# A hybrid decoder layer: two small casts change engines, and a scan's second tile gets a scheduling step of its own

## The chip, the cores and the metric

The kernel runs on one core of a Trainium2 chip. A core has engines that work side by side, each through its own queue in order: TensorE (PE in the profile; its weight loads are PEld), VectorE (DVE), ScalarE (ACT), GpSimd (POOL), and SyncE (SP), which here only issues DMA transfers. They wait for each other through semaphores. PE reads from SBUF and writes to PSUM; DVE and ACT read and write both. The metric is the time of one execution on the device in microseconds (us); a run's time is compared with others as a median of several.

## What is computed

One layer of a decoder over 16 meta tokens and 512 tokens, 1024 wide, in float32. Cut to what matters here:

```python
u = rmsnorm(h, mix_norm_w)
proj = u @ w_in                      # pool, z, xbc, dt, gates
xbc = silu(causal_depthwise_conv(xbc, conv_w, conv_b))        # 4 taps
xs, b_mat, c_mat = split(xbc)        # 32 heads of 64; 8 groups of state 128
dt = softplus(dt_raw + dt_bias);  a = -exp(a_log)
# chunks of 128 tokens, the 16 meta tokens a leading chunk of their own
y_diag = einsum("bclsg,bclsgr,bcsgrp->bclgrp", c.b, exp(a_l - a_s), x*dt)
states = einsum("bclgn,bclgr,bclgrp->bcgrpn", b, exp(a_end - a), x*dt)
prev   = scan over chunks: h = chunk_decay * h + states
y_off  = einsum("bclgn,bcgrpn,bclgr->bclgrp", c, prev, exp(a))
y = y_diag + y_off + xs * d_skip
yg = y * silu(z);  yg = yg * rsqrt(mean(yg**2 over the group) + eps) * norm_w
h = h + (gate_pool * y_pool + gate_ssd * (yg @ w_ssd_out)) @ w_o
h = h + relu(rmsnorm(h) @ w_ff1)**2 @ w_ff2
```

y_pool is a causal mean over 2 to 16 tokens, less the token itself, through two matrices. The output is the normalised h without the meta tokens.

## The kernel before

Matrices are multiplied with operands in two parts: a value rounded to the matrix type (`hi`, made by a cast on ACT) and what is missing (`lo`, a subtraction on DVE); three products of these (`whi`, `wlo` for a block of weights, `uh`, `ul` for the activations) make one. A block of weights is 128 x 1024; `block_part` (lines 72 to 76) loads it into `raw` (three buffers), casts it (L75) and subtracts (L76).

The scan goes group by group (eight groups of four heads), in the loop at lines 577 to 583. While the scan of group g is computed, the projections of group g+1 fill PE. Both are Python generators, `ssd` and `group_proj`, and `weave` takes one step of each in turn: a step ends at a `yield`. `group_proj` has a step for each of its tiles: bt (B), ct (C), the two halves of xc (x), then, for groups 1, 2, 3 and 5, a gate (pgp), and z (two blocks into pz, silu into zt). A tile's projection (px) ends in its convolution, `conv`: one tap on ACT (L340), three on DVE (L343), which read px in PSUM, and a silu on ACT (L345). For g = 4 the first half of the output projection (pso) is filled in as well, with two steps to one of the scan; for g = 7 the fill is the output projection of groups 4 to 6 (psp, `out_part`).

The steps of `ssd`:

1. abc, the running sums of the decay, is loaded and spread over the partitions. Transposes on PE: ptb (B in tokens; btok, bm), ptm and ptx (x in tokens; xdm, xm, xdt). The meta tokens' operands are stacked three times into 80 partitions: `bm` as hi, hi, lo and `xm` as hi, mid, hi, so that one product gives the sum of three. xdd is xdt times a decay; eb and abc are exponentials on ACT.
2. pcb = B times C, masked into cbm; the chunk states: pst from bm and xm for the meta tokens (L462), from btok and xdd for three chunks (L464); st is the running state (L466 on ACT, L468 and L469 on DVE); abc is multiplied with cbm (L470).
3. po = states times C (L478), py = xdt times abc (L484), each in two tiles; then four DVE instructions on each tile, the additions: yt = po * eb, + py, + xc * d_skip, * zt (L488 to L492).
4. The group norm: sq (L496, L497), its two parts qh and ql.
5. png, a sum over partitions by PE (L501, L502); the root rs on ACT (L504), four reciprocals on DVE (L506).
6. yt times norm weight and rs (L510); yh and yl, its two parts for the output projection (L513, L514).

What order the instructions take on each engine isn't the program's order. The Tile framework's scheduler works through the whole program with estimates of its own and puts an instruction into its engine's queue when it finds it ready; program order only gives the priority. So a `yield` that moves changes the priority of all that stands behind it. On the chip the queue is fixed, and an instruction that waits holds up all behind it on its engine.

PSUM has two buffers of two banks (px, pz, pso, psp, pgp) and four of one bank (ptb, ptm, ptx, pcb, pst, po, py, png). ACT loads a table (ACT_TABLE_LOAD) whenever its next function needs another one: root, exponential, silu and sigmoid each change it here.

Of the kernel before, what the change touches and what calls it, by code (L numbers as in the profile page):

```python
# [51 lines left out]
def kernel(ctx: ExitStack, tc, xT, x, w, vec, fnw, out):  # L52
    nc = tc.nc
    act, dve, pe, pool = nc.scalar, nc.vector, nc.tensor, nc.gpsimd
# [77 lines left out]
    xm = gc.tile([MQ, R, HEAD], F32R, name="xm", bufs=1)  # L132
# [55 lines left out]
    b, raw, hi, lo = wdt  # L188
# [200 lines left out]
    def bc(ap, n):  # L389
        return ap.unsqueeze(len(ap.shape)).to_broadcast(list(ap.shape) + [n])  # L390

    def ssd(g, cur):
# [10 lines left out]
        xdm = gs.tile([NM, R, 64], F32, tag="xdm", name=f"xdm{g}")  # L403
# [6 lines left out]
        hi, mid, low = slice(0, NM), slice(32, 32 + NM), slice(64, 64 + NM)  # L410
# [5 lines left out]
        for i in range(2):  # L416
            pe.transpose(pm[:NM, i * P : (i + 1) * P], xc[:, i, :NM], ident)
        dve.tensor_tensor(xdm, pm[:NM, :256].rearrange("p (r d) -> p r d", r=R),
                          bc(decm[:, hs], 64), op=ALU.mult)
        act.copy(xm[hi], xdm)  # L420
        act.copy(xm[low], xdm)
        dve.tensor_tensor(xm[mid], xdm, xm[hi].bitcast(F32), op=ALU.subtract)
        for b in range(2):
            pt = psum1(f"ptx{g}_{b}")
# [61 lines left out]
        for i in range(2):  # L486
# [3 lines left out]
            dve.scalar_tensor_tensor(y, xc[:, i, NM:], col(V_DS, 2 * g + i), y,  # L490
                                     op0=ALU.mult, op1=ALU.add)
            dve.tensor_tensor(y, y, zt[:, i, :], op=ALU.mult)  # L492
        yield

        sq = gs.tile([P, 2, SEQ], F32, tag="eb", name=f"sqg{g}")
        act.activation(sq, yt, AF.Square)  # L496
# [80 lines left out]
    for g in range(G):  # L577
        nxt = group_tiles(g + 1) if g + 1 < G else None
        fill = [group_proj(g + 1, nxt, GATE_AT.get(g))] if nxt else [out_part()]
        if g == 4:  # L580
            fill = [out_half()] + fill
        weave(ssd(g, cur), fill, 2 if g == 4 else 1)
        cur = nxt
# [638 lines left out]
```

## Time and profile before

| what | value |
|---|---|
| median of 3 runs | 1037.89 us (1037.26 to 1038.09) |
| profiled execution | 1037.43 us |
| its span, first to last instruction | 1035.7 us |
| mean granted clock of PE | 0.996 |
| the scan's groups (the weave) | about 66 to 500 us of the span |

In the page, a group of instructions is named by line, engine, operation and out<-in with the program's tile names; buffer numbers are left out, so px is any projection. A time line's row has start, duration, engine, line, operation, tiles, shapes, count, and in square brackets the idle time of the engine just before it and who ended it. A row of waits has the total, how often, and the longest. In a row of windows each engine has its busy time and its count; behind POOL stand the granted clock of PE, the DMA share and GB/s.

### The profile page before, as it was taken

Reading aid. Unit: us, or ns where it says so; the run is one execution under the profiler, and the core shown is the slowest. Engines: PE = TensorE matmul, PEld = TensorE weight load, DVE = VectorE, ACT = ScalarE, POOL = GpSimd, SP = SyncE. Lnnn points to the kernel's source line nnn. Section 1 sums busy time; section 2 is a strip of 40 time slices with the busy share of each in tenths; the row PEclk is TensorE's granted clock in tenths of the full one; section 3 lists DMA queues with packets and bytes.
Section 4 is the critical chain, followed back from the end, with each engine's and each line's share of the span. In section 5 each row is a group of like instructions: output and inputs, shape, how many; then the busy total and the mean of one; then the engine's idle time right before and its main releaser. Section 6 shows DMA issues by size and latency. Waiting matters only on the chain.

```text
span 1035.7 us, 14112 instructions
## 1 busy us (share of the span) xinstructions
PE 1011.8 (98%) x5689; PEld 875.4 (85%) x5689; DVE 737.1 (71%) x966; ACT 565.2 (55%) x756; POOL 88.6 (9%) x52
## 2 busy tenths in 40 slices
PE   9999899989899998999999999999999999999997
PEld 9889899879689997988899888888888888888886
DVE  7978787768645585878656557875777667666866
ACT  7776757667736439493234333465455345454444
POOL 0100000000000000000000000102131412403400
PEclk9999999999999999999999999999999999999999
DMA  6243142222233330504623333324323323334112
GB/s 237 84 143 102 32 132 84 100 87 97 84 123 100 90 113 2 166 18 122 224 85 99 102 102 87 137 68 156 102 82 122 102 83 121 97 107 119 43 43 82
DMA packets 29282, 105.64 MB, mean 102 GB/s; under 512 B 3296, under 2 KB 4256, under 8 KB 28192
## 3 DMA queue, kind: packets, MB, share of 16 engines
q1 hardware_dynamic: 26496, 92.75, 28.0%
q0 software_dynamic: 2000, 11.08, 3.0%
q8 instruction: 45, 0.74, 0.3%
q10 hardware_dynamic: 720, 0.91, 0.2%
q14 instruction: 21, 0.17, 0.0%
HBM read 102.55 MB, written 2.16 MB: 101 GB/s over the span
## 4 chain that ended last, share of the span: by engine, by line
PE 84%; ACT 9%; DVE 4%; issue 2%; DMA 0%; DVEq 0%; ACTq 0%
PE pf L93 6%; PE pf L92 6%; PE pf L94 6%; PE px L150 5%; PE px L153 5%; PE px L151 5%; PE alpha L971 3%; PE alpha L972 3%; PE alpha L973 3%; PE py L484 2%; PE pz L153 2%; PE pz L150 2%; PE pz L151 2%; PE pp L153 1%; PE pp L151 1%
## 5 line engine op out<-in xcount | busy, mean ns | idle before, releaser
L75 ACT CAST whi<-raw 128x1024 fp32r<-128x1024 f32 (+1 forms) x131 | 135.6, 1042 | 220.8 <-PE pf L93 55.8
L76 DVE TENSOR_TENSOR wlo<-raw,whi 128x1024 fp32r<-128x1024 f32 (+1 forms) x131 | 163.6, 1253 | 106.1 <-ACT whi L75 106.0
L150 PE MATMUL px<-uh,whi 128*128 128x264 f32 (+1 forms) x448 | 120.4, 289 | 5.9 <-ACT whi L75 3.0
L151 PE MATMUL px<-ul,whi 128*128 128x264 f32 (+1 forms) x448 | 118.0, 284 | 0.0
L92 PE MATMUL pf<-vh,whi 128*128 128x512 f32 x256 | 99.8, 390 | 0.0
L94 PE MATMUL pf<-vh,wlo 128*128 128x512 f32 x256 | 99.6, 389 | 0.0
L93 PE MATMUL pf<-vl,whi 128*128 128x512 f32 x256 | 99.6, 389 | 0.0
L150 PEld LDWEIGHTS px<-uh,whi 128*128 128x128 f32 x448 | 84.9, 189 | 9.0 <-ACT whi L75 4.8
L153 PE MATMUL px<-uh,wlo 128*128 128x264 f32 (+1 forms) x448 | 90.7, 285 | 1.1 <-DVE wlo L76 1.1
L151 PEld LDWEIGHTS px<-ul,whi 128*128 128x128 f32 x448 | 84.7, 189 | 0.3 <-issue 0.2
L733 DVE TENSOR_TENSOR slo<-b,shi 128x1024 fp32r<-128x1024 f32 x35 | 49.2, 1405 | 31.6 <-ACT shi L732 31.6
L153 PEld LDWEIGHTS px<-uh,wlo 128*128 128x128 f32 x448 | 68.7, 188 | 2.0 <-DVE wlo L76 1.5
L732 ACT CAST shi<-b 128x1024 fp32r<-128x1024 f32 x35 | 36.7, 1048 | 47.3 <-PE pf L93 36.4
L94 PEld LDWEIGHTS pf<-vh,wlo 128*128 128x128 f32 x256 | 48.0, 188 | 10.1
L92 PEld LDWEIGHTS pf<-vh,whi 128*128 128x128 f32 x256 | 48.0, 188 | 10.0
L93 PEld LDWEIGHTS pf<-vl,whi 128*128 128x128 f32 x256 | 48.1, 188 | 9.9
L982 POOL TENSOR_TENSOR b<-b,b 128x1024 f32<-128x1024 f32 x14 | 35.6, 2540 | 238.4 <-DVE slo L733 210.2
L971 PE MATMUL alpha<-shi,hh 128*128 128x512 f32 x140 | 54.6, 390 | 0.0
L972 PE MATMUL alpha<-slo,hh 128*128 128x512 f32 x140 | 54.5, 389 | 0.0
L973 PE MATMUL alpha<-shi,hl 128*128 128x512 f32 x140 | 54.5, 389 | 0.0
L798 DVE TENSOR_TENSOR ht<-ht,alpha 128x1024 f32<-128x1024 f32 x35 | 42.6, 1217 | 10.9 <-PE alpha L973 10.9
L150 PE MATMUL pz<-uh,whi 128*128 128x512 f32 x112 | 43.9, 392 | 0.0
(419 smaller groups left out, 2527.8 us busy)
## 6 DMA issues: line engine op xcount, KB each, us to landing
raw<-in_w SPq DMA_DIRECT2D x129, 512.0 KB, 3.6
b<-in_w SPq DMA_DIRECT2D x28, 512.0 KB, 3.6
abc<-acs_d POOLq DMA_DIRECT2D x8, 1024.0 KB, 5.0
wob<-in_w SPq DMA_DIRECT2D x8, 512.0 KB, 6.0
xt<-in_xT SPq DMA_DIRECT2D x8, 264.0 KB, 5.3
ht<-in_x POOLq DMA_DIRECT2D x4, 512.0 KB, 6.3
w<-in_w SPq DMA_DIRECT2D x4, 512.0 KB, 3.5
out_dram<-out SPq DMA_DIRECT2D x4, 320.0 KB, 2.4
```

Of the source, the lines that this page charges most:

```text
L75: act.copy(hi[:, c], raw[:, c])
L76: dve.tensor_tensor(lo[:, c], raw[:, c], hi[:, c].bitcast(F32), op=ALU.subtract)
L92: pe.matmul(ps, ah, bh, start=first, stop=False)
L93: pe.matmul(ps, ah, bl, start=False, stop=False)
L94: pe.matmul(ps, al, bh, start=False, stop=last)
L150: pe.matmul(o, wh, rhs[0][k][:, c], start=k == 0, stop=False)
L151: pe.matmul(o, wh, rhs[1][k][:, c], start=False, stop=False)
L153: pe.matmul(o, wl, rhs[0][k][:, c], start=False, stop=k == NK - 1)
L733: dve.tensor_tensor(lo, src, hi.bitcast(F32), op=ALU.subtract)
L971: pe.matmul(ps[t], a[0], wh[:, cs], start=f, stop=False, skip_group_check=True)
L972: pe.matmul(ps[t], a[0], wl[:, cs], start=False, stop=False, skip_group_check=True)
L973: pe.matmul(ps[t], a[1], wh[:, cs], start=False, stop=l, skip_group_check=True)
```

## The change

Two edits in `ssd`. The two casts of xdm into `xm` (lines 420 and 421) are issued by DVE instead of ACT. And the `yield` behind the additions moves into their loop, so that the step ends after the additions of tile 0 and again after those of tile 1: the scan has seven steps instead of six, and everything from the second tile's additions on comes one step of the fill later.

```diff
@@ -417,8 +417,8 @@
         dve.tensor_tensor(xdm, pm[:NM, :256].rearrange("p (r d) -> p r d", r=R),
                           bc(decm[:, hs], 64), op=ALU.mult)
-        act.copy(xm[hi], xdm)
-        act.copy(xm[low], xdm)
+        dve.tensor_copy(xm[hi], xdm)
+        dve.tensor_copy(xm[low], xdm)
         dve.tensor_tensor(xm[mid], xdm, xm[hi].bitcast(F32), op=ALU.subtract)
@@ -490,7 +490,7 @@
             dve.scalar_tensor_tensor(y, xc[:, i, NM:], col(V_DS, 2 * g + i), y,
                                      op0=ALU.mult, op1=ALU.add)
             dve.tensor_tensor(y, y, zt[:, i, :], op=ALU.mult)
-        yield
+            yield
 
         sq = gs.tile([P, 2, SEQ], F32, tag="eb", name=f"sqg{g}")
```

What the scheduler makes of it, in the instruction order. Names carry buffer numbers here: rs0 is group 0's root, xdm1 group 1's operand, whi17 the weight block of number 17. First ACT where the scan of group 0 ends and that of group 1 begins. Before, from the root of group 0 on:

```order
L504 ACT_TABLE_LOAD
L504 ACTIVATE rs0_1192<-png0_1189,eps_83 128x512
L439 ACT_TABLE_LOAD
L439 ACTIVATE eb1_1309<-abc1_1274 64x1024
L345 ACT_TABLE_LOAD
L345 ACTIVATE xc1_820<-xc1_820 128x528
L444 ACTIVATE abc1_1274<-abc1_1274,dtok_87 128x128 x3
L513 CAST yh0_0_1261<-yt0_1025 128x512
L385 ACTIVATE zt1_823<-pz1_1198 128x1024
L513 CAST yh0_1_1266<-yt0_1025 128x512
L409 COPY btok1_1278<-ptb1_1279 128x384
L412 CAST bm_114<-ptb1_1279 16x128
```

Now the root stands behind the exponential of abc and behind zt, and ahead of it stand the same table load and eb as above, and one Relu:

```order
L345 ACT_TABLE_LOAD
L345 ACTIVATE xc1_820<-xc1_820 128x528
L444 ACTIVATE abc1_1274<-abc1_1274,dtok_87 128x128 x7
L450 ACT_TABLE_LOAD
L450 ACTIVATE abc1_1274<-abc1_1274 128x1024
L385 ACT_TABLE_LOAD
L385 ACTIVATE zt1_823<-pz1_1189 128x1024
L504 ACT_TABLE_LOAD
L504 ACTIVATE rs0_1254<-png0_1251,eps_83 128x512
L409 COPY btok1_1278<-ptb1_1279 128x384
L412 CAST bm_114<-ptb1_1279 16x128
L413 CAST bm_114<-ptb1_1279 16x128
```

The root has moved behind eb, xc, the exponential of abc and zt, each with its table load. Next DVE at the same place. Before, from the subtraction that completes bm to the first state sum:

```order
L414 TENSOR_TENSOR bm_114<-ptb1_1279,bm_114 16x128
L422 TENSOR_TENSOR xm_115<-xdm1_1277,xm_115 16x256
L429 TENSOR_TENSOR xdt1_1276<-ptx1_1_1301,dtok_87 128x512
L447 TENSOR_SCALAR abc1_1274<-abc1_1274,dtok_87 128x128
L433 TENSOR_TENSOR xdd1_1307<-xdt1_1276,dec_89 128x768
L457 TENSOR_TENSOR cbm1_1395<-pcb1_1390,tri_78 128x512
L343 SCALAR_TENSOR_TENSOR bt2_1271<-px2_18_1330,vs_85,bt2_1271 128x527
L470 TENSOR_TENSOR abc1_1274<-abc1_1274,cbm1_1395 128x2048
L343 SCALAR_TENSOR_TENSOR bt2_1271<-px2_18_1330,vs_85,bt2_1271 128x526
L468 TENSOR_TENSOR st1_1_1398<-st0_1_1397,cdec_90 128x256
L343 SCALAR_TENSOR_TENSOR bt2_1271<-px2_18_1330,vs_85,bt2_1271 128x525
L469 TENSOR_TENSOR st1_1_1398<-st1_1_1398,pst1_0_1401 128x256
```

Now, to the same state sum:

```order
L506 RECIPROCAL rs0_1254<-rs0_1254 128x128 x4
L414 TENSOR_TENSOR bm_114<-ptb1_1279,bm_114 16x128
L510 SCALAR_TENSOR_TENSOR yt0_1025<-yt0_1025,vs_85,rs0_1254 128x512 x2
L343 SCALAR_TENSOR_TENSOR bt2_1271<-px2_18_1330,vs_85,bt2_1271 128x527
L514 TENSOR_TENSOR yl0_0_1262<-yt0_1025,yh0_0_1261 128x512
L514 TENSOR_TENSOR yl0_1_1267<-yt0_1025,yh0_1_1266 128x512
L343 SCALAR_TENSOR_TENSOR bt2_1271<-px2_18_1330,vs_85,bt2_1271 128x526
L457 TENSOR_TENSOR cbm1_1395<-pcb1_1390,tri_78 128x512
L343 SCALAR_TENSOR_TENSOR bt2_1271<-px2_18_1330,vs_85,bt2_1271 128x525
L468 TENSOR_TENSOR st1_1_1398<-st0_1_1397,cdec_90 128x256
L470 TENSOR_TENSOR abc1_1274<-abc1_1274,cbm1_1395 128x2048
L469 TENSOR_TENSOR st1_1_1398<-st1_1_1398,pst1_0_1401 128x256
```

The norm of group 0 (L506, L510, L514), which stood ahead of all this, stands in the middle of it. Where group 6 ends and group 7 begins the two engines change in the same way. Last, DVE where the gated group 2 ends and group 3 begins. Before:

```order
L514 TENSOR_TENSOR yl2_0_2164<-yt2_1957,yh2_0_2163 128x512
L514 TENSOR_TENSOR yl2_1_2169<-yt2_1957,yh2_1_2168 128x512
L414 TENSOR_TENSOR bm_114<-ptb3_2243,bm_114 16x128
L418 TENSOR_TENSOR xdm3_2241<-ptm3_2252,decm_91 16x256
L429 TENSOR_TENSOR xdt3_2240<-ptx3_0_2259,dtok_87 128x512
L429 TENSOR_TENSOR xdt3_2240<-ptx3_1_2265,dtok_87 128x512
L457 TENSOR_TENSOR cbm3_2359<-pcb3_2354,tri_78 128x512
L433 TENSOR_TENSOR xdd3_2271<-xdt3_2240,dec_89 128x768
L422 TENSOR_TENSOR xm_115<-xdm3_2241,xm_115 16x256
```

Now:

```order
L418 TENSOR_TENSOR xdm3_2241<-ptm3_2252,decm_91 16x256
L429 TENSOR_TENSOR xdt3_2240<-ptx3_0_2259,dtok_87 128x512
L514 TENSOR_TENSOR yl2_0_2226<-yt2_1957,yh2_0_2225 128x512
L420 CAST xm_115<-xdm3_2241 16x256
L421 CAST xm_115<-xdm3_2241 16x256
L422 TENSOR_TENSOR xm_115<-xdm3_2241,xm_115 16x256
L429 TENSOR_TENSOR xdt3_2240<-ptx3_1_2265,dtok_87 128x512
L457 TENSOR_TENSOR cbm3_2359<-pcb3_2354,tri_78 128x512
L514 TENSOR_TENSOR yl2_1_2231<-yt2_1957,yh2_1_2230 128x512
L433 TENSOR_TENSOR xdd3_2271<-xdt3_2240,dec_89 128x768
```

xm is complete four instructions earlier, behind two casts of its own, and both yl have moved from ahead of xdm to ahead of xdd. On PE the products for png (L501, L502) stand behind the next projection of the fill. At group 7's start six products of psp with group 6's yh and yl, which stood ahead of pst, stand behind it. Table loads on ACT rise from 62 to 66. From the end of the scan on, the order is the same, but for the place of a few loads (wob) on SP.

## The prediction

> **What bounds the kernel now.** I read the page's busy shares first, then the waits of TensorE alone, then the granted clock around those waits, then the time line of each engine at the places that the new order changes.
>
> ```profile
> span 1035.7 us, 14112 instructions
> PE 1011.8 (98%) x5689; PEld 875.4 (85%) x5689; DVE 737.1 (71%) x966; ACT 565.2 (55%) x756; POOL 88.6 (9%) x52
> ```
>
> TensorE (PE) works 98% of the span. Only what lengthens or shortens one of its few waits changes the time, some 24 us in all. The waits, longest first:
>
> ```profile
> PE pst L462 <- DVE xm L422: 6.6, 3, 2.2
> PE px L150 <- DVE bt L343: 2.7, 1, 2.7
> PE psp L94 <- DVE wlo L76: 0.9, 1, 0.9
> ```
>
> Columns: total us, times, longest. All lie where one group's scan ends and the next begins. A wait can cost more than its length. The next rows are stretches of 3.41 us: PE busy first, and behind POOL the granted clock.
>
> ```profile
> 119.82:123.24 3.42, 0.87 (x8) 0.67 (x6) 3.42 (x5) 1.78 (x2) 0.00 (x0) 1.00 0.00 0
> 123.24:126.65 3.41, 3.28 (x18) 2.95 (x18) 3.41 (x6) 1.93 (x2) 0.00 (x0) 0.50 0.21 35
> 215.38:218.79 3.41, 1.66 (x7) 1.18 (x7) 1.04 (x3) 3.36 (x6) 0.00 (x0) 1.00 0.00 0
> 266.60:270.01 3.41, 1.22 (x10) 1.03 (x10) 2.75 (x5) 3.36 (x5) 0.00 (x0) 1.00 0.00 0
> ```
>
> After a stretch with PE busy for 0.87 us of 3.42 the clock is halved for the next 3.41 us (second row); the same happens after 266.60 to 270.01, with 1.22 us busy. After 1.66 us busy (third row) it isn't. So a stretch that is idle for about 2 us or more costs up to 3.41 x 0.5 = 1.7 us on top. The Trainium skill ("TensorE: Matmul & The Clock Gate", section "What's actually happening") says that this window is 3413 ns long and runs freely, whatever the kernel does. The trace agrees: its two dips begin 146.77 us apart, 43 windows.
>
> **The change, part by part.** *What the extra yield moves.* It was to put the second tile's additions behind a convolution; the instruction order shows them moved by at most a row or two, since that order isn't the program's. What moves is all that comes behind: the group norm (png, its square root on ACT, the reciprocals, yt times norm, yh, yl) starts one projection later, and at the ends of the ungated groups 0 and 6 that is behind the gate projection z, the last of the fill. There it runs into the next group's first step.
>
> *Group 0 to 1, ACT.* Rows of before (durations; where rows of one engine follow without a wait, the next starts up to 0.09 us before the last one's end, and I take that off):
>
> ```profile
> 100.60 0.78 ACT L340 ACTIVATE xc<-px,vs 128x528 f32<-128x528 f32 x1
> 101.39 1.28 ACT L504 ACT_TABLE_LOAD   x1
> 102.69 0.69 ACT L504 ACTIVATE rs<-png,eps 128x512 f32<-128x512 f32 x1
> ...
> 104.69 1.06 ACT L439 ACTIVATE eb<-abc 64x1024 f32<-64x1024 f32 x1
> ...
> 107.06 0.65 ACT L345 ACTIVATE xc<-xc 128x528 f32<-128x528 f32 x1
> ...
> 109.74 1.02 ACT L385 ACTIVATE zt<-pz 128x1024 f32<-128x1024 f32 x1 [0.65 <-PE pz L153]
> ...
> 111.17 0.48 ACT L409 COPY btok<-ptb 128x384 f32<-128x384 f32 x1
> 111.54 0.25 ACT L412 CAST bm<-ptb 16x128 fp32r<-16x128 f32 x1
> ...
> 112.94 1.57 ACT L444 ACTIVATE abc<-abc,dtok 128x128 f32<-128x128 f32 x5
> ```
>
> Before, the norm's root rs is ready at 102.69 + 0.69 = 103.38. In the new order these stand between the same xc (end 101.38) and rs: five table loads (5 x 1.28), two exponentials of the size of eb (2 x 1.06), the silu of xc (0.65), eight Relus (8 x 0.31), zt (1.02) and the root (0.69): 13.4 us, so rs at about 114.8. Table loads rise by four in all (ACT's list in the order: 62 to 66), 5.1 us of an engine that is 55% busy.
>
> *The same place, VectorE (DVE).* Its rows, then those of PE that wait on them:
>
> ```profile
> 103.69 3.38 DVE L506 RECIPROCAL rs<-rs 128x128 f32<-128x128 f32 x4
> ...
> 107.11 1.42 DVE L510 SCALAR_TENSOR_TENSOR yt<-yt,vs,rs 128x512 f32<-128x512 f32 x2
> ...
> 111.44 0.68 DVE L514 TENSOR_TENSOR yl<-yt,yh 128x512 fp32r<-128x512 f32 x1
> 112.15 0.28 DVE L414 TENSOR_TENSOR bm<-ptb,bm 16x128 fp32r<-16x128 f32 x1
> ...
> 117.97 0.69 DVE L457 TENSOR_TENSOR cbm<-pcb,tri 128x512 f32<-128x512 f32 x1 [3.26 <-PE pcb L455]
> ...
> 119.25 2.28 DVE L470 TENSOR_TENSOR abc<-abc,cbm 128x2048 f32<-128x2048 f32 x1
> ...
> 122.46 0.76 DVE L343 SCALAR_TENSOR_TENSOR bt<-px,vs,bt 128x525 f32<-128x525 f32 x1
> 123.14 0.41 DVE L469 TENSOR_TENSOR st<-st,pst 128x256 f32<-128x256 f32 x1
> ```
>
> ```profile
> 117.69 0.36 PE L462 MATMUL pst<-xm,bm 80*128 80x256 f32 x1
> ...
> 123.37 0.56 PE L150 MATMUL px<-uh,whi 128*128 128x264 f32 x1 [2.68 <-DVE bt L343]
> 124.38 1.06 PE L478 MATMUL po<-ct,st 128*128 128x128 f32 x4
> ```
>
> In the new order the reciprocals stand ahead of bm's subtraction, and both yt products, both yl and cbm between bm and the state sums. With rs at 114.8: reciprocals to 118.1, bm to 118.4 (pst starts 0.7 us later than its 117.69), yt to 119.7, then two taps of bt, two yl, cbm and the third tap to 123.7 (px is released 0.5 us later), st's product 0.33, abc 2.2, and the state sum ends at about 126.6 where it ended at 123.55. PE's po, at 124.38 before, then waits to about 126.7: +2.3 us. Some of it comes back, since the half clock, which costs PE most of its 3.41 us now, would run out partly while it waits. I take +1.9, between 0.5 (px alone) and 3.1 (the whole delay of the sum).
>
> *Group 6 to 7* has the same order on ACT and DVE:
>
> ```profile
> 444.81 0.78 ACT L340 ACTIVATE xc<-px,vs 128x528 f32<-128x528 f32 x1
> ```
>
> ```profile
> 460.06 0.36 PE L462 MATMUL pst<-xm,bm 80*128 80x256 f32 x1
> ```
>
> 445.59 + 13.4 = 459.0 for rs, reciprocals to 462.3, bm to 462.6: pst at 462.65, a wait of 2.6 where there is none now. PE has nothing to put there: psp's products of the same group's yh and yl, which stand ahead of pst before, are themselves late now and stand behind it. Shorter waits on yh and st follow (some 0.6); the wait of 0.9 on wlo goes, as wlo moves ahead. +2.2.
>
> *The casts of xm* leave ACT (sixteen) and go to DVE. No row has a 16x256 cast there; the nearest are the one small cast on DVE, and as the upper end the 0.41 of the subtraction in the next fence, of the same size:
>
> ```profile
> L102 DVE CAST ones_r<-ones_f x1: 350/350/350, 1.1 to 1.1; 128x128 fp32r<-128x128 f32 x1
> ```
>
> I take 0.35 each; 0.2 would be the low end (half the elements' time of that subtraction). They matter at the ends of groups 2, 3 and 5, where pst waits 2.2 us for xm. At group 2 to 3:
>
> ```profile
> 215.95 0.41 DVE L422 TENSOR_TENSOR xm<-xdm,xm 16x256 fp32r<-16x256 f32 x1
> 218.70 2.29 DVE L470 TENSOR_TENSOR abc<-abc,cbm 128x2048 f32<-128x2048 f32 x1 [2.33 <-ACT abc L449]
> ```
>
> ```profile
> 215.49 0.39 ACT L420 CAST xm<-xdm 16x256 fp32r<-16x256 f32 x1
> ...
> 218.57 1.03 ACT L75 CAST whi<-raw 128x1024 fp32r<-128x1024 f32 x1
> ```
>
> ```profile
> 216.51 0.36 PE L462 MATMUL pst<-xm,bm 80*128 80x256 f32 x1 [2.19 <-DVE xm L422]
> ...
> 219.66 0.39 PE L150 MATMUL px<-uh,whi 128*128 128x264 f32 x1 [1.49 <-ACT whi L75]
> ...
> 222.18 0.51 PE L153 MATMUL px<-uh,wlo 128*128 128x264 f32 x2 [0.57 <-DVE wlo L76]
> ```
>
> The casts no longer stand behind zt's silu, so xm is ready at about 215.4, a microsecond sooner. But DVE now has two casts and both yl ahead of xdd, which pst's second product needs: before, xdd's and xm's seven instructions end at 216.36; with 2 x 0.61 and 2 x 0.35 more they end at 218.3. So pst's wait splits into about 1.1 and 2.6 us, px starts 0.2 us later instead of earlier, and only the end of the row, the wait on wlo, gains: ACT is some 0.7 us sooner with the last exponential (two casts of 0.4 less), abc and wlo then come 0.3 us sooner. -0.3 at each of the three, -1.0; the ends are +0.2 (px's start decides) and -0.7 (ACT's two casts).
>
> *The clock.* A wait of 2.6 us, with 1.1 close ahead of it, leaves a window under 1.3 us busy for most phases: I expect the dip at most of the three gated ends, where one of three has it now, and at group 6 to 7 in about half of the phases. That is two new dips; of 1.7 us each, some is spent in waits, so 1.2: +2.4, between 0 and 4 x 1.7 = 6.8. The Trainium skill (same page, section "HAM oscillation — how this bites in real kernels") has it that only idle gaps of more than about 3.4 us bring the slow clock. This trace says otherwise: 2.68 and 2.19 us were enough. By that rule this term would be nothing.
>
> *At no cost:* group 1's end and group 4's, where PE has no wait now and projections of ready weights lie over the norm; group 7's, whose yh is used only much later. If that cover went, each would cost what group 6's end does. SP's loads of wob move behind one raw load; they are used several blocks on.
>
> **The sum.** 1.9 + 2.2 - 1.0 + 2.4 = +5.5 us on the profiled execution. That took 1037.43 us, its span and 1.7 around it, 0.46 less than the median shown: 1037.89 + 5.5 = 1043.4, and I say 1043.0, since I may have the half clock at group 0's end twice. About 0.2%, 2.1 us, can be told from no change.
>
> **The rivals.** *No new dips:* the shorter waits fall across windows, and the clock stays. Then 1.9 + 2.2 - 1.0 = +3.1, 1041.0; the third clock row, idle for half its window and not slowed, speaks for it; the two others against. The skill's rule above would come out here. 22%.
> *Every dip:* four new ones at full price, 3.1 + 6.8 = +9.9, 1047.8. 6%.
> *Nothing that PE feels:* the additions hardly move, and the later norm is covered. That needs rs at group 0's end by 111.7, 3.1 us sooner than my sum (by 114.0 only pst, at 117.69, is covered; po waits on): then within 1 us of 1037.9. Against it: ACT has one wait between 101.4 and 113, of 0.65 us, so its queue has nothing to take back. 12%.
> *Faster:* xm's casts decide after all. If xdd ended by 217.5 instead of 218.3, pst would be done when whi is, px would start 0.7 us sooner at three places, and the dip after 270.01 would go (1.7): 3 x 0.7 + 1.7 = 3.8, and 1034.1 if groups 0 and 6 cost nothing as well. It takes casts of 0.2 us or less, and yl ready without a wait for yh. Against it: in the new order the second yh stands on ACT behind zt's silu. 8%.
>
> **Chances.** The forecast, +3.5 to +8: 52%. With the two rivals above, slower by over 0.2% holds 0.80, within 0.2% 0.12, faster 0.08. The range takes the no-dip case and its low end, 1.9 down to 0.5 and 2.2 down to 1.5, -1.0: 1038.5; above, three dips with the ends of group 0: 1047.
>
> **What would show it.** Right: TensorE's waits list pst for bm or xdd instead of xm, twice with 2.5 us; po at group 1 waits for st; ACT's table loads are 66; more halved windows. Wrong: pst waits nowhere, rs of group 0 ready by 111, or clock dips still two with gaps over 2 us. It would be wrong as a whole if ACT reached the late root sooner than my 13.4 us.

## The result, and the profile after

The changed kernel takes 1044.21 us (median, 1043.67 to 1045.25); the kernel before, run beside it, 1037.99 us. The ratio is 1.0062, with a 95% interval from 1.0044 to 1.0079: slower by 6.2 us. In a later set it was 1.0063 (1.0050 to 1.0075).

The page of the changed kernel, span and busy time:

```profile
span 1042.2 us, 14107 instructions
PE 1015.7 (97%) x5689; PEld 880.9 (85%) x5689; DVE 741.5 (71%) x982; ACT 564.8 (54%) x744; POOL 88.7 (9%) x52
```

The same 5689 matmuls keep TensorE (PE) busy for 3.9 us longer than before, in a span that is 6.5 us longer. So more than half of the loss isn't waiting: the same matmuls take longer, and the halved clock further down is why. PE's waits (total us, times, longest):

```profile
PE pst L464 <- DVE xdd L433: 7.0, 3, 2.3
PE pst L462 <- DVE xm L422: 3.3, 3, 1.1
PE pst L462 <- DVE bm L414: 3.2, 2, 2.6
PE po L478 <- DVE st L469: 2.7, 3, 2.0
PE po L478 <- DVE cbm L457: 2.2, 1, 2.2
```

Before, pst waited for xm alone, three times 2.2 us. Now, at the ends of groups 2, 3 and 5, it waits for xm 1.1 us and for xdd 2.3; at the end of group 6 for bm 2.6; and at the end of group 0 for bm, cbm and st in a row. PE's granted clock (behind POOL) around three of these places, in stretches that lie on the borders of the clock's own windows:

```profile
123.04:126.46 3.42, 1.22 (x6) 0.84 (x6) 3.42 (x4) 2.11 (x3) 0.00 (x0) 1.00 0.00 0
126.46:129.87 3.41, 2.68 (x15) 2.13 (x15) 3.41 (x6) 0.00 (x0) 0.00 (x0) 0.50 0.20 22
129.87:133.28 3.41, 3.41 (x17) 3.41 (x17) 2.51 (x5) 1.04 (x1) 0.00 (x0) 0.50 0.83 277
218.61:222.03 3.42, 0.36 (x1) 0.19 (x1) 3.33 (x7) 3.39 (x5) 0.00 (x0) 1.00 0.00 0
222.03:225.44 3.41, 3.16 (x8) 2.62 (x9) 3.41 (x3) 2.90 (x5) 0.00 (x0) 0.50 0.00 0
464.37:467.79 3.42, 0.84 (x5) 0.72 (x5) 3.36 (x6) 3.41 (x4) 0.00 (x0) 1.00 0.00 0
467.79:471.20 3.41, 3.41 (x11) 2.75 (x10) 3.41 (x5) 2.66 (x5) 0.00 (x0) 0.50 0.21 47
```

Six windows are halved ahead of the last one of the span (those of 276.64 and 416.59 us besides these four), where the kernel before had two. At the end of group 0 the window behind the first halved one is halved too. In the profile of the later set there were eight: where a wait falls on the windows' grid differs from execution to execution.

The time lines give the start of each group's first ptb transpose, and of the first product (pp) behind the scan. Their distances divide the scan into stretches, each named by the group ends in it. The differences to before, stretch by stretch, and in the last column the time at half clock ahead of the span's last window (all in us):

| kernel | ends of 0 and 1 | end of 2 | ends of 3 and 4 | end of 5 | end of 6 | halved |
|---|---|---|---|---|---|---|
| before | 0 | 0 | 0 | 0 | 0 | 6.8 |
| the change | +3.8 | +0.2 | -0.5 | +0.3 | +2.3 | 20.5 |
| the change, later set | +2.6 | +1.1 | +0.6 | +0.2 | +2.3 | 27.3 |
| casts alone | -3.8 | -0.7 | -0.8 | -0.7 | -1.8 | 3.4 |
| additions alone | +3.6 | -0.1 | -0.5 | +1.1 | +5.3 | 20.5 |
| the change, filled fully | +1.6 | -0.5 | -0.7 | -0.7 | +1.1 | 0 |

The last three rows are experiments.

### The profile page after: what moved, and what is told of

The parts are those of the page before. It is cut to its first block, busy times and chain, and to the rows that moved or that the text cites. A ratio compares the mean times of both kernels' runs of the same rounds, so it can differ in the third digit from the quotient of the medians.

```text
span 1042.2 us, 14107 instructions
## 1 busy us (share of the span) xinstructions
PE 1015.7 (97%) x5689; PEld 880.9 (85%) x5689; DVE 741.5 (71%) x982; ACT 564.8 (54%) x744; POOL 88.7 (9%) x52
## 4 chain that ended last, share of the span: by engine, by line
PE 84%; DVE 6%; ACT 6%; issue 2%; DMA 0%; SPq 0%; ACTq 0%; DVEq 0%
PE pf L94 6%; PE pf L92 6%; PE pf L93 6%; PE px L150 4%; PE px L151 4%; PE px L153 4%; PE alpha L971 3%; PE alpha L973 3%; PE alpha L972 3%; PE py L484 2%; PE pz L153 2%; PE pz L150 2%; PE pz L151 2%; PE pso L92 2%; PE pp L153 1%
```

## The experiments

The theory to test was the prediction's: the later additions cost at the ends of groups 0 and 6, the casts gain a little, and the clock's halved windows add to it. Its rivals were that the casts cost, that the loss is spread over all ends, and that such short waits don't touch the clock. All differences below are to the kernel before as run in the same set (1038.0 to 1039.0 us).

### Which part costs

*The casts alone:*

```diff
-        act.copy(xm[hi], xdm)
-        act.copy(xm[low], xdm)
+        dve.tensor_copy(xm[hi], xdm)
+        dve.tensor_copy(xm[low], xdm)
```

> The two casts of xm stand on VectorE, as in the changed kernel; the second scan tile's additions stay where they stood before. Our theory (the later additions cost, the casts don't): the three gated group ends are about 0.8 us shorter each, the ends of groups 0 and 6 stay as before, and a halved clock window more or less is worth about 1 us: 1037 us (1035.5 to 1038.5), so no loss. Rival (the casts on VectorE cost, by delaying xdd and what VectorE has behind it): most of the changed kernel's 6 us are here too, 1041 us or more.

Measured: 1031.51 us, -7.5; ratio 0.9925 (0.9912 to 0.9939). Neither theory had that: half of the change alone is a clear gain.

*The additions alone*, the casts on ScalarE (ACT) as before:

```diff
             dve.tensor_tensor(y, y, zt[:, i, :], op=ALU.mult)
-        yield
+            yield
```

> The fourth corner: the additions moved, the casts left on ScalarE. In the runs so far the casts alone took 7.5 us off, and the moved additions, with the casts already made, added 13.7 (1031.5 to the changed kernel's 6.2 above the kernel before). Theory one (the two parts are separate and simply add): before + 13 us, 1052 us (1049 to 1054). Theory two (the casts' gain is a better order of VectorE that a later norm undoes or gives too): the moved additions alone cost what the whole change costs, before + 6 us, 1045 us (1043 to 1047).

Measured: 1047.47 us, +9.5; 1.0092 (1.0076 to 1.0107), between the two theories and in neither one's range. More than half of it is at the end of group 6 (+5.3 in the table), where PE waits once 3.7 us for whi, a cast on ACT; the change doesn't have that wait. The parts don't add: -7.5 and +9.5 would make +2.0, and together they make +6.2 to +6.9. Of the casts' gain only 2.6 to 3.3 us are left once the additions are moved.

*The additions at the ends of groups 0 and 6 only*, with the casts:

```diff
             dve.tensor_tensor(y, y, zt[:, i, :], op=ALU.mult)
-            yield
+            if i or g in (0, 6):
+                yield
```

> The changed kernel with the additions moved back only at the ends of groups 0 and 6; at the ends of the others the first half of the group's output steps is left together, as before. Our theory (two group ends carry the loss): end of group 0 about +4.0 us, end of group 6 about +2.3, the gated ends about -0.8 each before their clock: 1044 us (1042.5 to 1045), the same as the changed kernel. Rival (the loss is spread over all the ends, by ScalarE's table loads or VectorE's order): about 1040 us.

*The additions at all the other ends*, with the casts (the same lines with `g not in (0, 6)`):

> The counterpart: the changed kernel with the additions moved back at every group end but those of groups 0 and 6. Our theory: what is left is the casts and six moves that nothing waits for: 1037.5 us (1036 to 1039.5). Rival (loss spread over all ends): about 1041 us. With the run that moves them at groups 0 and 6 alone the two differences from the kernel before should add up to the changed kernel's 6.2 us within 1.5 us.

*The additions at the end of group 0 only*, with the casts (`g == 0`):

> The casts on VectorE and the later additions at the end of group 0 alone. Theory one (group 0's end carries the larger part): the run with groups 0 and 6 stood 11 us above the run with the casts alone, of which its trace puts 8 at the end of group 0: 1039.5 us (1038 to 1041). Theory two (it is half and half with group 6): 1037 us. Theory three (group 6's end carries it): 1034 us.

Measured, in this order: 1042.62 us (1.0032, 1.0020 to 1.0045), 1032.11 us (0.9930, 0.9918 to 0.9943) and 1038.34 us (0.9995, 0.9986 to 1.0003). The second is far below both of its theories, and the first two differences add up to -3.3 us (+3.6 and -6.9) instead of the 6.2 expected, because both runs hold the casts' gain, which no theory had. Counted from the casts alone, at 0.9925, the moved additions cost 0.70% or 7.3 us at the end of group 0 (0.9995), 0.37% or 3.8 us more at the end of group 6 (1.0032), and 0.05% or 0.5 us at the other ends when they are moved alone (0.9930). These make 11.6 of the 14.3 us between the casts alone and the change (1.0063 - 0.9925 = 1.38%). The last 2.7 us would come only when all are moved together, but four ratios of about 0.13% each way stand behind this figure, so it is uncertain by about as much as it is large. The traces show one thing that the small 0.5 us hides. With the additions moved at the other ends alone, the ends of groups 2 and 5 are 1.6 and 0.9 us longer than with the casts alone, about as in the change (0.9 to 1.8, and 0.9); but the end of group 1 is 1.7 us shorter, because a wait of PE for bm (1.77 us, with the casts alone) is gone there. The runs that move the additions at the end of group 0 don't have that wait with or without the other moves, so nothing offsets the loss in the change. So the two ends that the prediction named carry most of the loss, but it is counted from a kernel that has the casts' gain already, and at the end of group 0 it is in part that gain lost again.

### Why the casts gain

VectorE (DVE) at the end of group 0 with the casts alone:

```profile
118.18 0.69 DVE L457 TENSOR_TENSOR cbm<-pcb,tri 128x512 f32<-128x512 f32 x1 [1.54 <-PE pcb L455]
118.83 0.77 DVE L343 SCALAR_TENSOR_TENSOR bt<-px,vs,bt 128x527 f32<-128x527 f32 x1
119.51 0.42 DVE L468 TENSOR_TENSOR st<-st,cdec 128x256 f32<-128x256 f32 x1
119.84 0.76 DVE L343 SCALAR_TENSOR_TENSOR bt<-px,vs,bt 128x526 f32<-128x526 f32 x1
120.52 0.41 DVE L469 TENSOR_TENSOR st<-st,pst 128x256 f32<-128x256 f32 x1
120.85 0.76 DVE L343 SCALAR_TENSOR_TENSOR bt<-px,vs,bt 128x525 f32<-128x525 f32 x1
...
121.86 2.29 DVE L470 TENSOR_TENSOR abc<-abc,cbm 128x2048 f32<-128x2048 f32 x1
```

Before, the product abc, 2.28 us, stood between the first and the second tap of bt, and the third tap ended at 123.22; PE waited 2.68 us for it, and the window behind that wait was halved. Here the product has slipped behind the taps and the first state sum. The third tap ends at 121.61, and PE doesn't wait. That is a matter of order, not of the casts' 0.28 us each. To see whether order does it, the product was moved behind the taps in the kernel before, with the casts left on ACT:

```diff
+        if g == 1:
+            yield
         dve.tensor_tensor(dm, dm, cbm.unsqueeze(1).to_broadcast([P, R, 4, P]), op=ALU.mult)
-        yield
+        if g != 1:
+            yield
```

> The kernel before, with one step in another order: at group 1 the product of the decay tile by cbm (2.28 us on VectorE) is written behind the next yield, so that VectorE does it behind the taps of bt, as it does in the run with the casts alone on VectorE; the casts stay on ScalarE. Theory one (the 7.5 us of the casts come for the most part from this order, which lifts TensorE's wait of 2.68 us for bt and the halved window behind it): before - 4.5 us (3 to 6), 1033.5. Theory two (it is ScalarE's relief that counts): within 1 us of before.

Measured: 1035.10 us, -3.6; 0.9966 (0.9954 to 0.9978). Its trace has the whole of it at the ends of groups 0 and 1 (-3.7), as the casts alone have -3.8 there. DVE has the order that was meant, and PE goes on without the wait:

```profile
121.88 0.76 DVE L343 SCALAR_TENSOR_TENSOR bt<-px,vs,bt 128x525 f32<-128x525 f32 x1
122.55 0.41 DVE L469 TENSOR_TENSOR st<-st,pst 128x256 f32<-128x256 f32 x1
122.88 2.28 DVE L472 TENSOR_TENSOR abc<-abc,cbm 128x2048 f32<-128x2048 f32 x1
```

```profile
120.33 0.61 PE L481 MATMUL po<-ct,st 128*128 128x128 f32 x4
121.01 0.51 PE L153 MATMUL px<-uh,wlo 128*128 128x258 f32 x2
121.35 0.28 PE L150 MATMUL px<-uh,whi 128*128 128x258 f32 x1
...
128.92 0.39 PE L150 MATMUL px<-uh,whi 128*128 128x264 f32 x1
```

But the edit moved more than the product, since the scheduler orders every engine anew. Before, the first four products of the next tile (px of 264 columns) stand in PE's queue right behind po's first four, so PE waits there for the third tap of bt, and the last 44 products of ct's projection (258 columns) stand behind that wait. Here, and with the casts alone, all 44 stand ahead, and the next tile starts at 128.92 (127.57 with the casts alone). DVE makes the first wlo that they need ahead of the last two taps (at 119.73; at 115.42 with the casts alone; before, at 123.46, behind all three). The third tap itself ends only 0.58 us sooner than before, at 122.64. If PE's order had stayed, PE would still have waited for it, about 1.7 us from the end of po at 120.94 on (an estimate from these rows). All runs with this gain (this one, the next one, the casts alone, also filled, and the casts with the additions at the other ends) have the 44 products ahead; the change and all runs with the additions moved at the end of group 0 have them behind, as before.

So about half of the casts' gain is shown to be the new order at this place, on PE and DVE together; the product's place alone was not tested. The other half lies at the ends of groups 2 to 6, 0.7 to 1.8 us a stretch. What makes it there was not taken apart; px's waits for whi, a cast on ACT, fall from 3.0 us in all to 1.0, and the next run shows that no work on DVE is needed.

*Without the casts* (left out in all groups but the first, so two of the three parts of xm are those of group 0):

```diff
+        if g == 0:
             act.copy(xm[hi], xdm)
             act.copy(xm[low], xdm)
```

> The kernel before, with the two casts of xm left out in every group but the first (the later groups use the first group's rounded xm in two of its three parts, so this part of the computation is left out). TensorE's and ScalarE's instructions then stand in the same order as in the run with the casts alone on VectorE. Theory one (ScalarE's relief and the new order are the gain, the casts cost VectorE nothing that counts): within 1.5 us of that run, before - 7.5 us, so 1031.5 us (1030 to 1033). Theory two (VectorE has to be loaded for the better order): about the time before, 1038.5 us. If the casts on VectorE do cost something at the ends of groups 2, 3 and 5, this run is up to 3 x 0.6 us faster than that one.

Measured: 1032.57 us, -5.4; 0.9944 (0.9930 to 0.9958). This lies in theory one's range, with no casts of xm on DVE: what counts is ACT's relief and the order that follows from it. That this run is 0.2% slower than the casts alone, though it does less, is hardly beyond the noise, but it has a place in the traces. PE has the same order in both (DVE's differs a little at the end of group 1, too), while three windows are halved here and one there. At the end of group 1 one is halved after a window with 1.41 us of work, and the stretch of the ends of 0 and 1 is 1.6 us longer (-2.2 in place of -3.8); the ends of 3 and 4, with another, are 1.2 us longer (+0.3 in place of -0.8). Whether the windows are the whole of it was not tested. The first:

```profile
159.13:162.54 3.41, 1.41 (x11) 1.05 (x9) 3.14 (x6) 3.36 (x7) 0.00 (x0) 1.00 0.00 0
162.54:165.95 3.41, 3.33 (x11) 2.88 (x11) 3.41 (x3) 2.29 (x4) 0.00 (x0) 0.50 0.26 40
```

### What the clock costs

*The change, filled once:* PE's waits stay, but are filled with matmuls that write again what is there. No other engine's order changes.

```diff
+        for _ in range({1: 2, 7: 8}.get(g, 0)):
+            pe.matmul(pc[:, 3 * P :], bt[:, tok(3)], ct[:, ctok(3)], start=True, stop=True)
...
-        pe.matmul(pv[0], bm, flat(xm), start=True, stop=True)
+        for _ in range(11 if g in (3, 4, 6) else 1):
+            pe.matmul(pv[0], bm, flat(xm), start=True, stop=True)
```

> The changed kernel, and in its waits on TensorE at five group ends a matmul that has just run is run again with the same operands and the same result (pst's first product 11 times at the ends of groups 2, 3 and 5, pcb's last one 8 times more at the end of group 6 and twice more at the end of group 0). The order of VectorE, ScalarE and the queues stays; nothing waits less, TensorE is only busy in place of idle. Our theory (a window of 3.41 us with little work halves the clock of a later one, and that is about 4 us of the 6.2): the halved windows at about 222, 276, 416 and 467 us go, and with them about 3.5 us: 1040.7 us (1039.3 to 1042). Rival one (waits this short don't touch the clock, or the halved windows cost nothing): 1044.2 us (1043.2 to 1045.2), the same halved windows. Rival two (the repeats lie on the path): above 1045 us.

Measured: 1042.81 us, +3.8; 1.0034 (1.0022 to 1.0046), 3.0 us below the change by the ratios. That lies between theory one's range and rival one's, in neither. Of the four halved windows that were aimed at, two are gone (276 and 467 us); waits of 1.1 us stayed on both sides of the repeats, and the windows at 223 and 417.5 us with them. In its profile the window of 467 us is worth 1.2 us (end of group 6: +1.1 in place of +2.3), that of 276 us 0.15 (ends of 3 and 4: -0.6 in place of -0.5).

*The change, filled fully,* against the change once more:

```diff
+        for _ in range({3: 6, 4: 6, 6: 6, 7: 14, 1: 4}.get(g, 0)):
+            pe.matmul(pc[:, 3 * P :], bt[:, tok(3)], ct[:, ctok(3)], start=True, stop=True)
...
+        for _ in range({3: 22, 4: 22, 6: 22}.get(g, 1)):
             pe.matmul(pv[0], bm, flat(xm), start=True, stop=True)
...
+                for _ in range({(1, 0, 0): 18, (1, 1, 0): 8}.get((g, i, c), 1)):
                     pe.matmul(po[i][:, c * P : (c + 1) * P],
```

> The changed kernel once more, on the chip of the other runs of this set, as the base for the next one: before + 6.2 us (5 to 7.5).

> The changed kernel with its waits filled further than in the first filled run: pst's first product 22 times at the ends of groups 2, 3 and 5, pcb's last product 6 times more there, 14 times more at the end of group 6 and 4 times more at the end of group 0, and there po's first product 18 times and its first product of the second half 8 times; each repeat writes what is there already. The order of VectorE, ScalarE and the queues is that of the changed kernel. Theory one (halved windows cost TensorE time that lies on the path everywhere): no halved window is left, and the time falls by about 4 us below the changed kernel. Theory two (from the first filled run, where the halved window after 276 us went and the next group came only 0.15 us sooner, while that of 467 us gave 1.2: at the gated ends VectorE and ScalarE set the pace and the clock is hidden): -1.2 at the end of group 6, -1 to -3 at the end of group 0, nothing at the three others: 2 to 4 us below the changed kernel, and the starts of the groups show where. Theory three (the halved windows have another cause): they stay and the time with them.

Measured: the change 1044.91 us, +6.9; 1.0063 (1.0050 to 1.0075). Filled fully 1038.11 us, +0.1; 0.9999 (0.9991 to 1.0008). Extra work on an engine that is busy for 97% of the time takes 6.8 us off, the whole loss and more than the 4 us of theory one. The change in this set, and then the filled run, at the end of group 0:

```profile
120.54:123.96 3.42, 1.26 (x9) 0.96 (x7) 3.42 (x6) 2.61 (x4) 0.00 (x0) 1.00 0.00 0
123.96:127.37 3.41, 1.58 (x6) 1.20 (x6) 3.41 (x5) 1.93 (x2) 0.00 (x0) 0.50 0.00 0
```

```profile
120.00:123.40 3.40, 3.40 (x28) 3.27 (x28) 3.40 (x7) 3.40 (x6) 0.00 (x0) 1.00 0.00 0
123.40:126.80 3.40, 3.40 (x33) 3.40 (x32) 3.40 (x4) 2.02 (x3) 0.00 (x0) 1.00 0.00 0
```

No window of the filled run is halved but the last of the span. The five stretches of the table are shorter by 1.0, 1.6, 1.3, 0.9 and 1.2 us than in the change of the same set. Theory two of the expectation, that the clock is hidden at the three gated ends, falls: the stretches with these ends give 3.8 of these 6.0 us. The Trainium skill ("TensorE: Matmul & The Clock Gate", section "HAM oscillation — how this bites in real kernels") names idle gaps over about 3.4 us as what brings the slow clock back; here no wait of PE at these ends was longer than 2.6 us, and filling them removed 27.3 us of halved clock. By these traces shorter waits are enough.

*The kernel before, filled:*

```diff
+        for _ in range({3: 14, 4: 14, 6: 14}.get(g, 0)):
+            pe.matmul(pc[:, 3 * P :], bt[:, tok(3)], ct[:, ctok(3)], start=True, stop=True)
...
+                for _ in range({(1, 0, 0): 14}.get((g, i, c), 1)):
                     pe.matmul(po[i][:, c * P : (c + 1) * P],
```

> The kernel before with two kinds of waits filled: at the end of group 0 po's first product runs 14 times, at the ends of groups 2, 3 and 5 pcb's last one 14 times more; the output is the same. VectorE's order is that of before but for cbm, which comes behind xm at those three ends. Theory one (the kernel before pays for its two halved windows as the changed one does): no halved window is left; at the end of group 0 the wait of 2.68 us for bt stays and the window behind it gives 1 us, at the end of group 3 0.2 to 1, and xm is up to 0.7 us sooner at three ends, of which the wait for whi leaves little: before - 2 us (1 to 3.5). Theory two (its halved windows are hidden): within 0.7 us of before. The difference to the filled run of the changed kernel is what the waits alone cost in the change.

Measured: 1037.01 us, -1.5; 0.9985 (0.9976 to 0.9994). The gain is at the end of group 0 (-1.5 in the stretch), where the wait for bt is filled and the window behind it is no longer halved. One window at the end of group 3 still was in the profile, later than before's, and that stretch is 0.9 us longer. From filled to filled the change costs 0.9999 - 0.9985 = 0.14%, 1.5 us, give or take 1.3. That is about what its waits and its order cost; the rest of the 0.63%, 0.49% or 5.1 us (give or take 1.9), is halved clock. As one window was still halved in this run's profile, up to 0.9 us may belong to the waits instead.

*The casts alone, filled:*

```diff
+        for _ in range({3: 4, 4: 4, 6: 4}.get(g, 0)):
+            pe.matmul(pc[:, 3 * P :], bt[:, tok(3)], ct[:, ctok(3)], start=True, stop=True)
...
+        for _ in range({3: 16, 4: 16, 6: 16}.get(g, 1)):
             pe.matmul(pv[0], bm, flat(xm), start=True, stop=True)
```

> The kernel with the casts alone on VectorE, and TensorE's waits at the ends of groups 2, 3 and 5 filled with repeats of products that are there already (pst's first product 16 times, pcb's last one 4 times more); the output is the same. Theory one (each halved window costs 1 to 1.6 us there, as the filled runs of the changed kernel showed, and that run still had one): 0.8 to 2.5 us below that run, 1030 us (1028.5 to 1031), the fastest of all, and no halved window before the last. Theory two (with so few halved windows nothing is left to gain): within 0.7 us of 1031.5.

Measured: 1031.34 us, -7.4; 0.9927 (0.9915 to 0.9940), the same as the casts alone. Its clock is full up to the last window of the span, and yet nothing is gained. PE at the end of group 5 shows why; the casts alone first, at half clock from 407.19 to 410.60, then with the repeats:

```profile
408.04 0.59 PE L150 MATMUL px<-uh,whi 128*128 128x264 f32 x1 [0.26 <-ACT whi L75]
...
409.08 1.06 PE L478 MATMUL po<-ct,st 128*128 128x128 f32 x4
...
410.72 0.40 PE L153 MATMUL px<-uh,wlo 128*128 128x264 f32 x2
```

```profile
408.54 0.39 PE L150 MATMUL px<-uh,whi 128*128 128x264 f32 x1 [0.57 <-ACT whi L75]
...
409.13 0.61 PE L481 MATMUL po<-ct,st 128*128 128x128 f32 x4
...
411.07 0.39 PE L153 MATMUL px<-uh,wlo 128*128 128x264 f32 x1 [0.56 <-DVE wlo L76]
```

At full clock PE is through the same matmuls sooner and then waits 0.56 us for wlo. So a halved window costs only what no later wait takes back: nothing here, 1.5 us at the end of group 0 of the kernel before.

## Why the prediction was right, and where it was not

The forecast was +5.5 us on the profiled execution and 1043.0 us; measured were +6.2 us and 1044.21. The sign and the size hold, and most of the steps. But two terms were sized wrongly in opposite directions, so that the sum came this close is partly luck, and the two edits do not share the cost as the prediction had it.

- **The root and what follows it, group 0.** Predicted: rs at 114.8, reciprocals to 118.1, bm to 118.4, PE's po at about 126.7. ACT's row, DVE's and PE's of the change (its first ptb of group 1 stands 0.4 us later than before's):

```profile
114.57 0.69 ACT L504 ACTIVATE rs<-png,eps 128x512 f32<-128x512 f32 x1
```

```profile
115.30 3.39 DVE L506 RECIPROCAL rs<-rs 128x128 f32<-128x128 f32 x4 [0.72 <-ACT rs L504]
118.71 0.28 DVE L414 TENSOR_TENSOR bm<-ptb,bm 16x128 fp32r<-16x128 f32 x1
```

```profile
119.14 0.35 PE L462 MATMUL pst<-xm,bm 80*128 80x256 f32 x1 [0.63 <-DVE bm L414]
...
123.65 0.49 PE L478 MATMUL po<-ct,st 128*128 128x128 f32 x2 [2.16 <-DVE cbm L457]
...
127.19 1.22 PE L478 MATMUL po<-ct,st 128*128 128x128 f32 x4 [2.04 <-DVE st L469]
```

  rs ended at 115.26, the reciprocals at 118.69, bm at 118.99, and po came at 127.19: within 0.6 us of the sum at every step. A wait that the prediction didn't name is in it: po's second tile has to have one of the four one-bank PSUM buffers, and pcb's comes free only with cbm. The stretch is 3.8 and 2.6 us longer in the two profiles, not 1.9. Filled, without any halved window, it is 1.6 longer than before, which has one there; against before as filled, whose stretch is 1.5 shorter, it is 3.2. So the waits are at the upper end that the prediction gave (3.1), and it was right that before's half clock takes some of them back.
- **Group 6.** Predicted: a wait of pst for bm of 2.6 us, and +2.2. The wait was 2.58 and the stretch +2.3, but +1.1 when it was filled: half of the term was the clock, which the prediction had counted in its own term.
- **The gated ends.** Predicted: pst's wait splits into about 1.1 and 2.6 us, -0.3 at each. It split into 1.1 and 2.3. Filled, the three stretches give -0.5 to -0.7 each, a larger gain than predicted; with the halved windows, between -0.5 and +1.1.
- **The clock** is the mis-sized term. Predicted: two new halved windows, 1.2 us each, +2.4. There were four more in one profile and six more in the other, and between filled and filled the clock makes 5.1 us of the change (4.2 if the 0.9 us of the window left in the filled kernel before is the waits'). The waits, predicted at 1.9 + 2.2 - 1.0 = +3.1, make 1.5 (or 2.4). The sum came out because the two misses nearly cancel.
- **The rivals.** *No new dips* is out by the windows, *nothing that PE feels* by the waits. *Every dip* had the count of windows, four more and six more, but not their price: its 1047.8 us is 3.6 above the measured time. *Faster, since the casts decide* was told with the wrong mechanism (xdd at the gated ends) and given 8%; the casts do decide -7.5 us when they come alone. Not seen was that, alone, they change the order of PE and DVE at the end of group 0: the prediction compared before and the change only as a whole, and PE's order there is the same in both (ct's 44 products behind the next tile's first four), so this gain, which the moved additions undo, could not show. The additions cost 14.3 us on top of the casts, where the prediction put its whole cost of about 6 down to them.

The better version is half of the change: the casts on DVE, the `yield` where it was, 0.75% faster than before.

## What to carry to other kernels

Where a change has two edits, cost each against the kernel before, with its own instruction order; the sum of both can be right while each is far off, and the gain of one is lost. When one engine's order looks like the cause, compare the order of the others too. Where TensorE is busy for 98% of the time, a wait of 2 us can cost more than its length, here up to about 1.6 us more a stretch: look at the granted clock behind it, and count a halved window only where no later wait would take the time back. Repeating matmuls that write what is there already, inside the waits, is a quick test of what the clock costs; here it was worth 6.8 us.

## What the runs showed of the hardware

When PE's clock is halved can be read off the traces of all the profiled kernels here. Laid on the grid of 3.413 us that the clock's own steps show, some 4100 windows at full clock, the last few of each span left out: all 27 with PE busy for less than 1.54 us were followed by a halved window, of 32 between 1.54 and 2.2 us seven were, and none above 2.2. The busy time of the trace counts a matmul to its modelled end, which may be why the border is not sharp. Behind a halved window the clock came back 34 times, with 2.95 us busy or more; nine times, with 1.56 to 2.99 us, it stayed halved for another. So it isn't the length of one wait that counts but how much of a window is idle, and with waits of 2 us it is chance, from execution to execution, on which side a window falls. Two profiles of the changed kernel had 20.5 and 27.3 us of halved clock.
